# Three feed-forward tiles per down product, and the next block's factors made in steps and kept in HBM

## The chip, the cores and the metric

The kernel runs on one core of a Trainium2 chip. The metric is the device time of one execution in microseconds; the time given for a kernel is the median of its runs.

## The reference

One layer of a hybrid encoder trunk on 2048 tokens of width 1024: three token mixers and their output projection, then a gated feed-forward part with a convolution of width 3 over tokens. The change lies in the feed-forward part alone:

```python
D_MODEL = 1024
SEQ = 2048
D_FF = ((8 * D_MODEL // 3 + 127) // 128) * 128      # 2816, 22 tiles of 128
CONV_W = 3
...
def conv_glu_ffn(h, w_up, conv_w, conv_b, w_down):
    gate, val = jnp.split(h @ w_up, 2, axis=-1)
    t = gate.shape[1]
    gp = jnp.pad(gate, ((0, 0), (CONV_W - 1, 0), (0, 0)))
    conv = conv_b
    for i in range(CONV_W):
        conv = conv + gp[:, i:i + t] * conv_w[i]
    return (jax.nn.silu(conv) * val) @ w_down
...
        x = x + jnp.concatenate([ya, yb, yc], axis=-1) @ w_out[l]
        h = rms_norm(x, ffn_norm_g[l])
        x = x + conv_glu_ffn(h, w_up[l], conv_w[l], conv_b[l], w_down[l])
```

## The kernel before

The first stages (projections, the three mixers, the output projection) fill the first 1780 us or so. They leave x + mixers in HBM as x2D, features by tokens, and the inverse norms of all tokens in the tiles rsb. The feed-forward stage (line 1258 on) follows.

Tokens are worked in three blocks, `BL` (line 58): twice 344, then twice 340 and twice 340 tokens; the two halves of a block are the two halves of a Strassen-like scheme. Each f32 operand is split into a high and a low part (`split`, line 159: a cast on ScalarE to the high part, a subtraction on VectorE, or on another engine if one is named, for the low part), and each product of two operands is three matmuls: high-high, high-low, low-high.

Per block the right factors `Bs` (seven tiles B0 to B6, each of four row sets, high and low) hold sums and differences of the normalised x. `build` (line 1166) makes them: per row set j it scales two x tiles on VectorE (line 1172), takes four sums or differences on GpSimd (lines 1177 to 1180), and splits seven results into the B tiles (line 1182). It is a generator that yields after each split. The B tiles have one buffer each.

The loop (line 1356) runs over 22 tiles of 128 gate and 128 value columns. `up_w` loads a tile's weights into two of three raw buffers and makes four combined ones on GpSimd, a tile ahead. `ffn_up` (line 1289) takes seven products in the order 0, 1, 6, 2, 3, 4, 5, each 12 matmuls into one PSUM bank; before each product its weights are split into a wu tile (four buffers). VectorE combines the products; then come the convolution (lines 1320 and 1322), the silu, the gating (line 1324) and the split of the result into a hid tile.

`ffn_down` (line 1336) multiplies hid tiles by w_down for eight output tiles and two halves, a PSUM bank each, and adds each bank to acc on VectorE (line 1346). It takes G = 2 tiles at a time: after tiles 2, 4, ..., 18 the two earliest ready ones. `down_w` (line 1329) loads w_down rows into a raw buffer and splits them into a wd tile (two buffers), the low part on GpSimd. After the last tile, four are left: two groups of two, and the weights of the second group are loaded after the first group's products.

At the end of a block (lines 1369 to 1387) `build` for the next block runs interleaved with these last two groups, `PACE` = 1 step per output bank. Then acc goes to the output, and the next block loads its acc from x2D. All loads and stores of this stage are issued by SP.

The order of instructions on an engine is not that of the code: a scheduler places an instruction when its operands and buffers are there by its own reckoning, earlier code first. The semaphores follow from that order.

## Time and profile before

| | us |
|---|---|
| median of 3 runs (3209.77 to 3211.91) | 3211.55 |
| the profiled execution: its time | 3213.01 |
| its span | 3211.2 |
| TensorE busy (94%) | 3017.4 |
| VectorE busy (74%) | 2368.5 |
| ScalarE busy (43%) | 1394.9 |
| GpSimd busy (30%) | 950.1 |

The profile is one execution, recorded instruction by instruction. Its engines are PE (TensorE matmuls), PEld (TensorE weight loads, beside PE), DVE (VectorE), ACT (ScalarE), POOL (GpSimd) and SP, which issues most DMAs. A group of instructions is told by its line in the kernel, the engine, the operation, and out<-in by the program's names; "x132" is a count. Behind an arrow stands what ended the idle time before the instruction. The lines 160 and 161 belong to `split`, so there the tile's name tells which split it is. A window gives, for a stretch of the span, its length, the busy time of PE, PEld, DVE, ACT and POOL with their instruction counts, the granted TensorE clock as a share of full speed, the share of time in which the DMA engines were busy, and GB/s. Times are us from the span's start unless marked otherwise.

### The profile page before, as it was taken

What the parts mean: (1) busy time and instruction counts of PE and PEld (TensorE: products, weight loads), DVE (VectorE), ACT (ScalarE), POOL (GpSimd) and SP (SyncE); (2) the same over time, 40 slices, a digit from 0 to 9 for tenths busy, and PEclk for the clock granted to TensorE, in tenths of its full rate; (3) what the DMA queues carried; (4) which work ended last, traced back from release to release, by engine and by line L of the source; (5) the groups of instructions that cost most, each with busy time, mean ns of one, the idle gap of its engine ahead of it and who ended that gap; (6) DMA issues with size and microseconds to landing.
All of it is one profiled execution on the core that took longest, in us unless ns stands there. A gap on an engine that the chain in (4) does not pass through costs nothing.

```text
span 3211.2 us, 49128 instructions
## 1 busy us (share of the span) xinstructions
PE 3017.4 (94%) x17820; PEld 2638.9 (82%) x17820; DVE 2368.5 (74%) x4590; ACT 1394.9 (43%) x2610; POOL 950.1 (30%) x928
## 2 busy tenths in 40 slices
PE   6988989998999979999989999999999998999999
PEld 4766767776767756677789899998899998999998
DVE  6667666756676646777553788889988889988886
ACT  5434444544444335578532343334333334333332
POOL 1010010001001021144242444444444444444443
PEclk8988999999999989999999999999999999999999
DMA  7756755656644576523234322222422222422221
GB/s 223 213 154 179 207 165 150 175 151 177 171 120 125 143 177 152 139 73 86 73 103 151 132 79 80 79 69 77 158 79 80 79 79 81 136 73 79 79 80 68
DMA packets 310818, 392.92 MB, mean 122 GB/s; under 512 B 137144, under 2 KB 228804, under 8 KB 299752
## 3 DMA queue, kind: packets, MB, share of 16 engines
q1 hardware_dynamic: 305936, 378.44, 40.0%
q0 software_dynamic: 2816, 8.39, 0.9%
q10 hardware_dynamic: 1824, 2.95, 0.4%
q8 instruction: 141, 2.31, 0.3%
q14 instruction: 101, 0.83, 0.1%
HBM read 304.65 MB, written 86.36 MB: 122 GB/s over the span
## 4 chain that ended last, share of the span: by engine, by line
PE 67%; DVE 17%; issue 5%; ACT 4%; DMA 4%; POOL 2%; SPq 1%; POOLq 0%; DVEq 0%; ACTq 0%
PE ps L1299 7%; PE ps L1298 7%; PE ps L1297 7%; PE ps L1345 4%; PE ps L1343 4%; PE ps L1344 4%; PE mm L282 2%; PE mm L281 2%; PE mm L283 2%; PE o L1069 2%; DVE tm L533 2%; DVE T L536 2%; PE z L652 2%; PE ps L1205 2%; PE ps L1206 2%
## 5 line engine op out<-in xcount | busy, mean ns | idle before, releaser
L1299 PE MATMUL ps<-B,wu 128*128 128x340 f32 (+1 forms) x1848 | 594.0, 321 | 19.6 <-DVE wu L161 19.4
L1297 PE MATMUL ps<-B,wu 128*128 128x340 f32 (+1 forms) x1848 | 589.7, 319 | 1.9 <-ACT wu L160 1.8
L1298 PE MATMUL ps<-B,wu 128*128 128x340 f32 (+1 forms) x1848 | 590.5, 320 | 0.0
L1299 PEld LDWEIGHTS ps<-B,wu 128*128 128x128 f32 x1848 | 348.7, 189 | 27.9 <-DVE wu L161 27.5
L1343 PE MATMUL ps<-hid,wd 128*128 128x340 f32 (+1 forms) x1056 | 341.9, 324 | 13.4 <-ACT wd L160 10.2
L1297 PEld LDWEIGHTS ps<-B,wu 128*128 128x128 f32 x1848 | 348.7, 189 | 2.6 <-ACT wu L160 2.1
L1298 PEld LDWEIGHTS ps<-B,wu 128*128 128x128 f32 x1848 | 347.8, 188 | 0.1
L1345 PE MATMUL ps<-hid,wd 128*128 128x340 f32 (+1 forms) x1056 | 338.8, 322 | 3.8 <-POOL wd L161 3.7
L1344 PE MATMUL ps<-hid,wd 128*128 128x340 f32 (+1 forms) x1056 | 340.1, 322 | 0.0
L281 PE MATMUL mm<-hT,w 128*128 128x512 f32 x704 | 314.5, 447 | 22.4 <-ACT w L160 16.0
L161 DVE TENSOR_TENSOR wu<-S,wu 128x512 fp32r<-128x512 f32 x264 | 258.0, 984 | 74.3 <-ACT wu L160 74.3
L282 PE MATMUL mm<-hT,w 128*128 128x512 f32 x704 | 291.2, 414 | 7.8 <-DVE hT L161 6.6
L283 PE MATMUL mm<-hT,w 128*128 128x512 f32 x704 | 291.3, 414 | 1.2 <-DVE w L161 1.1
L1346 DVE TENSOR_TENSOR acc<-acc,ps 128x340 f32<-128x340 f32 (+1 forms) x528 | 247.1, 502 | 48.1 <-PE ps L1345 47.8
L161 POOL TENSOR_TENSOR wd<-raw,wd 128x1024 fp32r<-128x1024 f32 x66 | 171.3, 2618 | 269.4 <-ACT wd L160 267.8
L160 ACT CAST wu<-S 128x512 fp32r<-128x512 f32 x264 | 162.9, 618 | 151.2 <-PE ps L1299 140.7
L1343 PEld LDWEIGHTS ps<-hid,wd 128*128 128x128 f32 x1056 | 201.6, 191 | 16.4 <-ACT wd L160 11.1
L1345 PEld LDWEIGHTS ps<-hid,wd 128*128 128x128 f32 x1056 | 201.6, 191 | 6.1 <-POOL wd L161 6.1
L161 DVE TENSOR_TENSOR wu<-raw,wu 128x512 fp32r<-128x512 f32 x198 | 201.1, 1017 | 5.6 <-ACT wu L160 5.6
L1344 PEld LDWEIGHTS ps<-hid,wd 128*128 128x128 f32 x1056 | 201.8, 191 | 0.0
L281 PEld LDWEIGHTS mm<-hT,w 128*128 128x128 f32 x704 | 138.8, 197 | 66.9 <-ACT w L160 17.0
L160 ACT CAST wu<-raw 128x512 fp32r<-128x512 f32 x198 | 120.7, 620 | 162.0 <-PE ps L1299 142.1
(337 smaller groups left out, 6814.2 us busy)
## 6 DMA issues: line engine op xcount, KB each, us to landing
w<-wD SPq DMA_DIRECT2D x72, 1024.0 KB, 6.6
raw<-in_w_up_dram SPq DMA_DIRECT2D x132, 512.0 KB, 3.6
raw<-in_w_down_dram SPq DMA_DIRECT2D x66, 512.0 KB, 3.6
wD<-w SPq DMA_DIRECT2D x24, 1024.0 KB, 5.5
wraw<-in_w_in_dram SPq DMA_DIRECT2D x24, 512.0 KB, 6.3
xt<-in_xT_dram SPq DMA_DIRECT2D x48, 256.0 KB, 4.2
K<-qkD SPq DMA_DIRECT2D x21, 512.0 KB, 8.3
Q<-qkD SPq DMA_DIRECT2D x84, 128.0 KB, 2.9
```

The source lines that it names most:

```text
L160: (hi_eng or nc.scalar).copy(hi, src) if (hi_eng or nc.scalar) is nc.scalar else hi_eng.tensor_copy(out=hi, in_=src)
L161: (lo_eng or nc.vector).tensor_tensor(lo, src, f(hi), op=ALU.subtract)
L281: mm(ps, hi[:, kt, 0:P], hT[kt][:, 0, :], start=(kt == 0), stop=False)
L282: mm(ps, hi[:, kt, 0:P], hT[kt][:, 1, :], start=False, stop=False)
L283: mm(ps, lo[:, kt, 0:P], hT[kt][:, 0, :], start=False, stop=(kt == KT - 1))
L1297: mm(ps, whl[:, 0, kt, :], Bs[p][:, kt, 0, 0:n], start=(kt == 0), stop=False)
L1298: mm(ps, whl[:, 0, kt, :], Bs[p][:, kt, 1, 0:n], start=False, stop=False)
L1299: mm(ps, whl[:, 1, kt, :], Bs[p][:, kt, 0, 0:n], start=False, stop=(kt == 3))
L1343: mm(ps, wd[:, 0, ch], hid[:, 0, cs], start=(u == 0), stop=False)
L1344: mm(ps, wd[:, 0, ch], hid[:, 1, cs], start=False, stop=False)
L1345: mm(ps, wd[:, 1, ch], hid[:, 0, cs], start=False, stop=(u == G - 1))
L1346: nc.vector.tensor_tensor(acc[ct][:, cs], acc[ct][:, cs], ps, op=ALU.add)
```

## The change

`ffn_down` takes three tiles a group: tiles 0 to 2, ..., 15 to 17, then 18 and 19, and 20 and 21. A bank collects nine matmuls instead of six before it is added to acc. A group's down products follow the up products of the next group's first tile, so four tiles of up products come first in a block, then three between two down groups. wd has three buffers. The last pair's w_down is split into four wu tiles (`down_last`) instead of wd tiles.

The next block's factors are no longer built at the block's end into the B tiles. `build_ahead` makes them in small steps within the running block, from its third tile on, up to three steps per tile (before the matmuls of products 1, 2 and 4 of `ffn_up`), 48 steps in all: one step loads x tiles, two scale one each, two do two GpSimd operations each in x and in a tile that shares its buffer with TS, and seven split one result each into a tile st (two buffers) and store it in HBM (`kept`). At the block's end, when each B tile's last product is through, seven DMAs load the factors from HBM, in the order in which the products use them. x4 has two buffers instead of three, TS grows to 688 columns, and the scratch for DMA descriptors shrinks.

```diff
-BUFS = {"fr": 7, "bk": 4, "bp": 2, "fl": 6, "wraw": 2, "w": 3, "xt": 2, "pr": 3, "p2": 6, "vs": 1, "st": 4, "raw": 3, "yh": 5, "xr": 3, "tmp": 5, "wu": 4, "s4": 4, "hid": 4, "x4": 3, "vv": 1}
+BUFS = {"fr": 7, "bk": 4, "bp": 2, "fl": 6, "wraw": 2, "w": 3, "xt": 2, "pr": 3, "p2": 6, "vs": 1, "st": 4, "raw": 3, "yh": 5, "xr": 3, "tmp": 5, "wu": 4, "s4": 4, "hid": 4, "x4": 2, "vv": 1}
...
-    TSR = [(cA0.tile([P, 640], F32, name="TS"), cA0.tile([P, 256], F32, name="TR"))]
+    TSR = [(cA0.tile([P, 2 * HN], F32, name="TS", tag="TS")[:, 0:640], cA0.tile([P, 256], F32, name="TR"))]
...
-    wd4 = p4.enter_context(tc.tile_pool(name="wd4", bufs=2))
+    wd4 = p4.enter_context(tc.tile_pool(name="wd4", bufs=3))
...
-    G = 2
+    st4 = p4.enter_context(tc.tile_pool(name="st4", bufs=2))
+
+    GROUPS = [list(range(g, g + 3)) for g in range(0, NF - 4, 3)] + [[NF - 4, NF - 3], [NF - 2, NF - 1]]
...
+    def build_ahead(b, kept):
+
+        t1, n = BL[b]
+
+        def put(p, j, o):
+            t = st4.tile([P, 2, HN], F32R, name="st")
+            split(t[:, 0, 0:n], t[:, 1, 0:n], o)
+            nc.sync.dma_start(out=kept[p][:, j], in_=f(t[:, :, 0:n]))
+
+        for j in range(4):
+            hs = []
+            for kt in (j, j + 4):
+                h = x4.tile([P, 2 * HN], F32, name="x4")
+                nc.sync.dma_start(out=h[:, 0 : 2 * n], in_=x2D[kt * P : (kt + 1) * P, t1 : t1 + 2 * n])
+                hs.append(h)
+            yield
+            for kt, h in zip((j, j + 4), hs):
+                nc.vector.scalar_tensor_tensor(
+                    h[:, 0 : 2 * n], h[:, 0 : 2 * n], par("ffn_g", kt), rsb[b][:, 0 : 2 * n], op0=ALU.mult, op1=ALU.mult
+                )
+                yield
+            b11, b12, b21, b22 = hs[0][:, 0:n], hs[0][:, n : 2 * n], hs[1][:, 0:n], hs[1][:, n : 2 * n]
+            tt = cA0.tile([P, 2 * HN], F32, name="tt", tag="TS")
+            t2, t3 = tt[:, 0:n], tt[:, HN : HN + n]
+            nc.gpsimd.tensor_tensor(t3, b22, b12, op=ALU.subtract)
+            nc.gpsimd.tensor_tensor(t2, t3, b11, op=ALU.add)
+            yield
+            for p, o in ((0, b11), (1, b21), (2, t2)):
+                put(p, j, o)
+                yield
+            nc.gpsimd.tensor_tensor(b12, b12, b11, op=ALU.subtract)
+            nc.gpsimd.tensor_tensor(b21, t2, b21, op=ALU.subtract)
+            yield
+            for p, o in ((3, t3), (5, b22), (4, b12), (6, b21)):
+                put(p, j, o)
+                yield
 
...
-    def ffn_up(Bs, left, fi, n):
+    def ffn_up(Bs, left, fi, n, work):
...
+            if p in (1, 2, 4):
+                next(work, None)
...
-        return wd
+        return lambda s, ct: wd[:, s, ct * P : (ct + 1) * P]
+
+    def down_last(fis):
+
+        raws = []
+        for fi in fis:
+            raw = raw4([P, DM])
+            nc.sync.dma_start(out=raw, in_=w_down[fi * P : (fi + 1) * P, :])
+            raws.append(raw)
+        whl = [[ws4.tile([P, 2, 4, P], F32R, name="wu") for _ in fis] for h in range(2)]
+        for u, raw in enumerate(raws):
+            for h in range(2):
+                t = whl[h][u]
+                split(t[:, 0], t[:, 1], raw[:, h * 512 : h * 512 + 512].rearrange("p (a c) -> p a c", c=P), None, nc.gpsimd)
+        return [lambda s, ct, u=u: whl[ct // 4][u][:, s, ct % 4, :] for u in range(len(fis))]
 
     def ffn_down(acc, grp, n):
         for ct in range(KT):
-            ch = slice(ct * P, (ct + 1) * P)
             for hf in range(2):
                 cs = slice(hf * n, hf * n + n)
                 ps = bank()[:, 0:n]
                 for u, (hid, wd) in enumerate(grp):
-                    mm(ps, wd[:, 0, ch], hid[:, 0, cs], start=(u == 0), stop=False)
-                    mm(ps, wd[:, 0, ch], hid[:, 1, cs], start=False, stop=False)
-                    mm(ps, wd[:, 1, ch], hid[:, 0, cs], start=False, stop=(u == G - 1))
+                    mm(ps, wd(0, ct), hid[:, 0, cs], start=(u == 0), stop=False)
+                    mm(ps, wd(0, ct), hid[:, 1, cs], start=False, stop=False)
+                    mm(ps, wd(1, ct), hid[:, 0, cs], start=False, stop=(u == len(grp) - 1))
                 nc.vector.tensor_tensor(acc[ct][:, cs], acc[ct][:, cs], ps, op=ALU.add)
-                yield
 
     left_ = None
     for b, (t0, n) in enumerate(BL):
@@ -1352,39 +1405,34 @@
         acc = [a4.tile([P, 2 * HN], F32, name=f"acc{ct}") for ct in range(KT)]
         for ct in range(KT):
             nc.sync.dma_start(out=acc[ct][:, 0 : 2 * n], in_=x2D[ct * P : (ct + 1) * P, ts_])
-        ready, work = [], iter(())
+        work, more = iter(()), b + 1 < len(BL)
+        if more:
+            n1 = BL[b + 1][1]
+            kept = [dram.tile([P, 4, 2, n1], F32, name=f"BD{b}{p}") for p in range(7)]
+            work = build_ahead(b + 1, kept)
+        hids, g = {}, 0
         for fi in range(NF):
             left = left_ if left_ is not None else up_w(fi)
-            ready.append(ffn_up(Bs, left, fi, n))
+            hids[fi] = ffn_up(Bs, left, fi, n, work if fi > 1 else iter(()))
             if todo is not None:
                 todo()
                 todo = None
-            left_ = up_w((fi + 1) % NF) if fi + 1 < NF or b + 1 < len(BL) else None
-            if G < len(ready) and fi < NF - G:
-                for _ in ffn_down(acc, list(zip(ready, wds)), n):
-                    pass
-                ready = ready[G:]
-            if fi % G == 0 and fi < NF - G:
-                wds = [down_w(fi + u) for u in range(G)]
-        if b + 1 < len(BL):
-            t1, n1 = BL[b + 1]
-
-            def load(kt, t1=t1, n1=n1):
-                xt = x4.tile([P, 2 * HN], F32, name="x4")
-                nc.sync.dma_start(out=xt[:, 0 : 2 * n1], in_=x2D[kt * P : (kt + 1) * P, t1 : t1 + 2 * n1])
-                return xt
-
-            Bs = factors()
-            work = build(Bs, b + 1, load, tmp4)
-        while ready:
-            for _ in ffn_down(acc, list(zip(ready, wds)), n):
-                for _ in itertools.islice(work, PACE):
-                    pass
-            ready = ready[G:]
-            if ready:
-                wds = [down_w(NF - G + u) for u in range(G)]
+            left_ = up_w((fi + 1) % NF) if fi + 1 < NF or more else None
+            if fi == 0:
+                wds = [down_w(k) for k in GROUPS[0]]
+            elif g + 2 < len(GROUPS) and fi == GROUPS[g + 1][0]:
+                ffn_down(acc, [(hids.pop(k), w) for k, w in zip(GROUPS[g], wds)], n)
+                g += 1
+                wds = [down_w(k) for k in GROUPS[g]]
         for _ in work:
             pass
+        wdl = down_last(GROUPS[-1])
+        if more:
+            Bs = factors()
+            for p in (0, 1, 6, 2, 3, 4, 5):
+                nc.sync.dma_start(out=f(Bs[p][:, :, :, 0:n1]), in_=kept[p])
+        for ks, ws_ in zip(GROUPS[-2:], (wds, wdl)):
+            ffn_down(acc, [(hids.pop(k), w) for k, w in zip(ks, ws_)], n)
...
-    nc = _bacc.Bacc("TRN2", target_bir_lowering=False, num_devices=1, dynamic_dma_scratch_size=4096)
+    nc = _bacc.Bacc("TRN2", target_bir_lowering=False, num_devices=1, dynamic_dma_scratch_size=1024)
```

## Rows read from the trace of the kernel before

**Rows 1.** the page, part 1: engine, busy us (share), instructions
```profile
PE 3017.4 (94%) x17820; PEld 2638.9 (82%) x17820; DVE 2368.5 (74%) x4590; ACT 1394.9 (43%) x2610; POOL 950.1 (30%) x928
```

**Rows 2.** windows, feed-forward: stretch, its us, busy us per engine, PEclk, DMA
```profile
1850.00:2200.00 350.00, 350.00 (x2222) 350.00 (x2221) 299.14 (x435) 135.93 (x203) 164.59 (x121) 1.00 0.24 79
...
2800.00:3180.00 380.00, 380.00 (x2440) 380.00 (x2440) 326.88 (x482) 148.34 (x223) 168.78 (x126) 1.00 0.22 74
```

**Rows 3.** windows at the ends and starts of the three blocks
```profile
1780.00:1831.60 51.60, 44.42 (x256) 42.12 (x255) 44.25 (x58) 23.58 (x41) 26.83 (x18) 0.93 0.53 184
2179.70:2221.50 41.80, 40.44 (x254) 39.76 (x253) 36.50 (x45) 19.82 (x33) 24.76 (x19) 1.00 0.23 76
2221.50:2264.80 43.30, 36.36 (x193) 33.84 (x191) 40.42 (x65) 16.38 (x31) 21.69 (x20) 0.88 0.45 144
2264.90:2313.80 48.90, 42.21 (x253) 39.34 (x254) 47.76 (x57) 19.63 (x32) 27.19 (x19) 1.00 0.48 153
2657.90:2699.50 41.60, 40.15 (x254) 39.31 (x253) 36.42 (x45) 19.72 (x33) 24.73 (x19) 1.00 0.23 77
2699.50:2742.50 43.00, 35.57 (x194) 33.37 (x193) 40.12 (x65) 16.37 (x31) 22.40 (x20) 0.88 0.41 133
2742.50:2788.50 46.00, 41.32 (x254) 39.20 (x253) 43.59 (x54) 19.63 (x32) 25.04 (x19) 1.00 0.47 150
...
3132.60:3171.90 39.30, 39.30 (x254) 39.30 (x253) 33.02 (x46) 17.66 (x28) 19.90 (x13) 1.00 0.20 68
3171.90:3207.10 35.20, 32.30 (x193) 31.18 (x191) 19.03 (x36) 4.49 (x5) 4.89 (x3) 0.95 0.17 65
```

**Rows 4.** waits of PE from 2221.5 to 2264.8: who, us in total, times, longest
```profile
PE ps L1343 <- ACT wd L160: 4.8, 1, 4.8
```

**Rows 5.** groups on DVE, 2803.5 to 3180: count, busy us, mean ns, idle before
```profile
L1346 DVE TENSOR_TENSOR acc<-acc,ps 128x340 f32<-128x340 f32 x137 | 63.2, 501 | 9.8 <-PE ps L1345 9.8
```

**Rows 6.** timeline of DVE: start us, us, what [idle before]; two follow-on tiles
```profile
2762.62 2.78 DVE L1322 SCALAR_TENSOR_TENSOR cv<-gt,pps,cv 128x680 f32<-128x680 f32 x2
...
2777.89 2.80 DVE L1322 SCALAR_TENSOR_TENSOR cv<-gt,pps,cv 128x680 f32<-128x680 f32 x2 [0.43 <-ACT cv L1320]
```

**Rows 7.** timeline of DVE, last block: a split for the third follow-on tile
```profile
3159.14 0.68 DVE L161 TENSOR_TENSOR wu<-raw,wu 128x512 fp32r<-128x512 f32 x1
```

**Rows 8.** groups on DVE, 2200 to 2300: work on the next factors
```profile
L161 DVE TENSOR_TENSOR B<-u,B 128x340 fp32r<-128x340 f32 x16 | 13.7, 858 | 2.7 <-ACT B L160 2.7
...
L161 DVE TENSOR_TENSOR B<-x,B 128x340 fp32r<-128x340 f32 x12 | 10.5, 885 | 0.0
L1172 DVE SCALAR_TENSOR_TENSOR x<-x,pps,rsb 128x680 f32<-128x680 f32 x8 | 10.4, 1314 | 0.0
```

**Rows 9.** timeline of all engines from 2203.3: a POOL and a DVE row
```profile
2204.17 1.29 POOL L1286 TENSOR_TENSOR S<-raw,S 128x512 f32<-128x512 f32 x1 [1.48 <-DVE wu L161]
...
2204.37 1.64 DVE L161 TENSOR_TENSOR wu<-raw,wu 128x512 fp32r<-128x512 f32 x1
```

**Rows 10.** timeline of SP's DMA issues, block 0
```profile
1803.73 1.38 SPq L1374 DMA_DIRECT2D x<-x2D  x3
```

**Rows 11.** windows with DMA near its most
```profile
1800.00:1805.00 5.00, 5.00 (x32) 4.81 (x31) 4.53 (x10) 2.29 (x4) 0.58 (x1) 1.00 1.01 384
...
2750.00:2760.00 10.00, 10.00 (x67) 10.00 (x66) 8.77 (x13) 3.26 (x5) 6.59 (x5) 1.00 0.91 274
```

**Rows 12.** timeline of all engines, 2275 to 2283: a load and its cast
```profile
2275.55 0.33 SPq L1331 DMA_DIRECT2D raw<-in_w_down_dram  x1
...
2281.78 1.05 ACT L160 CAST wd<-raw 128x1024 fp32r<-128x1024 f32 x1 [3.31 <-DMA raw<-in_w_down_dram]
```

**Rows 13.** waits of SP's DMA queue, 1850 to 3211
```profile
SPq L1279 <- POOL wd L161: 473.5, 57, 15.6
```

**Rows 14.** the list of DMA issues: count, KB each, median us to landing
```profile
raw<-in_w_down_dram SPq DMA_DIRECT2D x66, 512.0 KB, 3.6
...
yD<-yl POOLq DMA_DIRECT2D x16, 256.0 KB, 3.7
```

## Prediction

> **What bounds the kernel now.** I read the page first: TensorE is busy for 94% of the span, VectorE for 74% [rows 1], so the question is where TensorE is not fed. The windows answer it: inside a token block of the feed-forward stage TensorE is busy for every microsecond, and the matmul counts give its pace, 350/2222 = 0.1575 us for 344 columns and 380/2440 = 0.1557 us for 340 [rows 2]. VectorE works 299 and 327 us of those 350 and 380 us (85 to 86%) and nobody waits for it there. The losses lie at the block ends. Three tiles' up products are 252 matmuls (39.7 us in block 0, 39.2 us after), the last four tiles' down products 192 (30.2 and 29.9 us). Against that the stretches of [rows 3] took, in order of time: block 0's first three tiles 51.6, 11.9 over; block 0's last three 41.8, 2.1 over; its last downs 43.3, 13.1 over; block 1's first three 48.9, 9.7 over; block 1's last three 41.6, 2.4 over; its last downs 43.0, 13.1 over; block 2's first three 46.0, 6.8 over; block 2's last three 39.3, 0.1 over; the closing downs 35.2, 5.3 over. Together 64.4 us, of which the two changes of block hold 24.9 and 22.3. Within the downs one wait of 4.8 us is for a cast of w_down [rows 4], which needs a buffer that the group before still reads; after it the granted clock of the stretch is 0.88. The rest is VectorE: busy 40.4 of 43.3 us and 47.8 of 48.9 us [rows 3], because it makes the next block's factors there.
>
> **The change, part by part.** (1) *Groups of three.* PSUM groups fall from 11 x 16 to 8 x 16 a block, so 3 x 48 = 144 additions to acc go, each 63.2/137 = 0.46 us [rows 5]: 66 us of VectorE. All of it lies beside down matmuls, where TensorE is full; credit 0. The price is that three tiles' up products now follow each other without a down between (four at a block's start). When VectorE sets the pace, one tile takes 2777.89 - 2762.62 = 15.27 us [rows 6] against 84 x 0.1557 = 13.08 us of matmuls, so it falls back 2.2 us a tile. What covers this is the lead of up to four split weights (wu has four buffers), 48 x 0.1557 = 7.5 us. How thin it gets, block 2's last three tiles show: the split for the third tile's second product ends at 3159.82 [rows 7], and TensorE, started at 3132.6, wants it at 3132.6 + 15 x 12 x 0.1557 = 3160.6. That run lost only 0.1 us, but its last tile prepares no following one. Block 2's five runs of three: between 0.1 and 2.2 each; I take 0.6, near the row that is most like them: 3 us. Block 0's fourth tile in its opening: between 0 and 2.2, since VectorE already sets the pace there; I take 1.5.
>
> (2) *Factors made in the running block.* Per block 28 splits (13.7 and 10.5 us) and 8 scalings of 1.31 us [rows 8]: 34.7 us of VectorE, besides 28 ScalarE casts and 16 GpSimd operations, twice. The nearest row is a run of three tiles that carried a quarter of it: blocks 0 and 1 already split one set of seven factors, with its four GpSimd operations, into their last three tiles, and these lost 2.1 and 2.4 us where the run without it lost 0.1 [rows 3]. Four sets a block at 2.25 make 9 us, 18 us for two blocks. Below, 0, if it falls into VectorE's free seventh; above, the first rival.
>
> The steps' 28 stores and the 7 loads add SP issues, 0.33 us each for a plain one [rows 12]. SP waits a lot: up to 15.6 us for a raw buffer [rows 13]. A store queued behind such a wait holds one of two st buffers; the third step's cast then waits on ScalarE, and the weight casts behind it, and then TensorE. A wait under the 7.5 us of lead costs nothing, the longest one 8 us. How often it meets a store the trace can't show; I take 0, since the stores are at least a product apart, and leave it in the range.
>
> (3) *The changes of block.* The last three tiles carry no step (48 steps, three a tile from the third, end with tile 17): 1 instead of 2.1 and 2.4, gain 2.5. In the last downs VectorE keeps only 32 additions, and the last pair's weights go to wu buffers, so the 4.8 us wait goes. Late next is the second of its raw loads or the seven factors. The factors are 7 x 1.39 = 9.75 MB, 25.4 us at 384 GB/s, 35.6 us at 274 [rows 11]; the first may start when tile 21's first product is through, 72 matmuls or 11.2 us before the downs, and the last is wanted some 11 us after them. So there are 52 us for 26 to 36. I take 2 us lost each, instead of 13.1: gain 22.2. Bounds 0 and the second rival.
>
> The next block's first tiles start without a backlog on VectorE, but with half the lead, because two of the four wu buffers come free only with the last down, and with four tiles in a row: I take 4 us each for 9.7 and 6.8, gain 8.5; bounds 0 and those rows.
>
> (4) *The end.* Its downs lose 1 instead of 5.3: gain 4.3, bounds 0 and 5.3. TS grown to 688 columns and x4 at two buffers: nothing waits for them. The smaller descriptor scratch can touch only the GpSimd-queue DMAs before this stage, such as the 16 of yD at 3.7 us [rows 14]; each has long before its reader comes; 0, at most one such landing.
>
> **The sum.** Gains 2.5 + 22.2 + 8.5 + 4.3 = 37.5; costs 3 + 1.5 + 18 = 22.5; net 15. The profiled execution took 3213.0 us, 1.5 above the median of 3211.55, so 3198 beside it and **3197** as a median. Its own range, with each taken value moved halfway to its bounds, is 3185 to 3207.
>
> **Rivals.** *A: VectorE is overrun in the runs of three.* Per run it falls back 3 x 2.2 = 6.6 us, and a fifth of 34.7 is 6.9 more. It decides from the point where the sum passes the 7.5 us of lead: 13.5 - 7.5 = 6.0 us in each of ten runs, 60 us instead of 18, the bare runs 0 instead of 3: 3197 + 39 = **3236**, slower. For it: the thin lead [rows 7] and GpSimd's part. A split that met a GpSimd operation took 1.64 us [rows 9], one that met none 0.68 [rows 7]; the change moves 16 such operations a block among the splits. The Trainium skill, SBUF — State Buffer, section Who interferes with whom, states that a VectorE instruction with two SBUF inputs contends with a GpSimd instruction that reads SBUF; by that rule, which the two rows agree with, spreading the steps can't hide them for free. It also covers the case that the change doesn't do what it says: instructions are not issued in the code's order (block 1's first x loads, due at its block's end, went out at 1803.73 [rows 10], over 400 us early), so the steps may bunch in the first seven tiles. Then VectorE has 7 x 15.27 + 16 x 0.46 + 34.7 = 149 us of work there, TensorE 7 x 13.08 + 22.4 = 114; less 7.5 of lead that is 27.5 a block instead of 9, again 3234. Against it: the runs with a quarter of the steps lost 2.1 and 2.4, not 6.
>
> *B: the last weight load queues behind the factors.* The second raw of the last pair can load only when the first is split, about the end of tile 21; by then most factor loads are out. If it lands after them, that is 25.4 to 35.6 us after a start 11.2 us before the downs, plus about 4 us for its own load, cast and first split: 18 to 28 us into the downs, wanted at 14.9. A stall of 3 to 13, 8 on the mean, and some 3 more at the lower clock as in [rows 3], 11 instead of 2, twice: 3197 + 18 = **3215**. For it: a w_down load issued among others at 2275.55 was cast at 2281.78 [rows 12], 6.2 us, where 3.6 is the median [rows 14]. The Trainium skill, DMA: Bandwidth & Descriptors, section Queues, rings and completion order, says that on each engine descriptors are consumed in ring order; by that rule, which those rows agree with, a load issued after the factors can't pass them. Against it: SP may issue it after four of the seven.
>
> *C: everything is covered.* The steps and bare runs cost 0 (21 us less) and the starts 2 instead of 4: **3172**.
>
> **How the numbers follow.** Chances: forecast 0.40, A 0.28, B 0.17, C 0.15. A measurement of this kernel tells 0.2%, 6.4 us, from no change, so faster means below 3205.1 and slower above 3218. Faster: 0.34 of the forecast, all of C, 0.04 of B: 0.53. Same: 0.05, 0.03 of A, 0.08 of B: 0.16. Slower: 0.01, 0.25 of A, 0.05 of B: 0.31. The range reaches from C to A, 3172 to 3238.
>
> **What would show it.** Windows of the changes of block: final downs near 32 us and first tiles losing some 4 us would show step 3 right; a TensorE wait for a wd or wu cast in the second half of the downs, with the factor loads still running, is B. Inside blocks 0 and 1 TensorE should lose 2 to 3 us per run to VectorE's splits; 6 in each, or long losses in the first seven tiles alone, is A. Block 2 without steps separates the price of the runs from that of the steps. The forecast is wrong if ScalarE waits for stores, or if TensorE waits for a factor's load at a block's start.

## Result and profile after

The changed kernel takes 3245.4 us (median of 4 runs, 3239.6 to 3247.8), the kernel before on the same chip 3211.7; the ratio is 1.0098, 95% interval 1.0078 to 1.0117. That is 1.0% slower, clear of the noise, and outside the forecast's range, on the side of rival A. The profiled run took 3239.6 us with a span of 3237.8, 26.6 us above before's.

The page's first part of after; it answers [rows 1]:

```profile
PE 3027.8 (94%) x17820; PEld 2638.8 (81%) x17820; DVE 2344.8 (72%) x4446; ACT 1385.7 (43%) x2616; POOL 975.6 (30%) x934
```

VectorE has the 144 instructions fewer (4590 - 4446) that the groups of three promised, 66 us by [rows 5], but its busy time fell by 23.7 only.

Windows of after, columns as in [rows 2] (stretch, its us, busy us of PE, PEld, DVE, ACT, POOL with counts, granted clock, DMA share, GB/s). The first two answer [rows 2], the others [rows 3]:

```profile
1850.00:2200.00 350.00, 328.12 (x2023) 319.48 (x2022) 297.16 (x404) 133.50 (x217) 170.12 (x127) 1.00 0.35 112
2800.00:3180.00 380.00, 374.03 (x2377) 370.11 (x2377) 312.26 (x423) 141.21 (x217) 173.20 (x126) 1.00 0.23 75
...
1783.80:1851.00 67.20, 58.47 (x338) 56.28 (x339) 62.02 (x84) 34.21 (x59) 43.51 (x29) 0.95 0.59 197
1873.60:1931.60 58.00, 44.84 (x255) 40.99 (x254) 53.49 (x66) 25.37 (x46) 37.60 (x27) 0.97 0.52 158
1954.30:2004.10 49.80, 42.77 (x254) 39.60 (x253) 44.12 (x54) 21.97 (x39) 33.65 (x23) 1.00 0.45 148
2026.70:2067.50 40.80, 40.26 (x255) 39.80 (x253) 37.34 (x43) 19.80 (x32) 28.47 (x19) 1.00 0.27 91
2258.50:2289.00 30.50, 30.50 (x194) 30.50 (x193) 20.89 (x40) 4.97 (x8) 5.77 (x6) 1.00 0.95 325
2289.00:2354.60 65.60, 56.22 (x338) 53.47 (x337) 57.17 (x63) 27.55 (x45) 35.48 (x25) 0.97 0.41 141
2731.60:2761.40 29.80, 29.80 (x193) 29.80 (x193) 20.43 (x40) 4.94 (x8) 5.72 (x6) 1.00 0.98 330
2761.40:2827.20 65.80, 58.77 (x338) 55.86 (x337) 56.94 (x63) 27.55 (x45) 35.06 (x25) 0.92 0.41 142
3203.90:3234.00 30.10, 30.10 (x193) 29.83 (x192) 19.40 (x36) 3.04 (x4) 2.20 (x3) 1.00 0.19 76
```

Read from below: the three last downs take 30.5, 29.8 and 30.1 us with TensorE full, where [rows 3] had 43.3, 43.0 and 35.2. This part did better than forecast: the factor loads, and the stores and loads of acc behind them, move 325 and 330 GB/s beside the downs, and TensorE waits for none of them. But TensorE is no longer full inside the blocks. The first three stretches of ups of block 0 (tiles 0 to 3, 4 to 6, 7 to 9) take 67.2, 58.0 and 49.8 us for 52.9, 39.7 and 39.7 us of matmuls, and the fourth is nearly clean, 40.8. The four-tile openings of blocks 1 and 2 take 65.6 and 65.8 us for 52.3.

What TensorE waits for in the whole stage is nearly one thing, VectorE's splits of the up weights (waits of PE, 1780 to 3238: who, us in total, times, longest):

```profile
PE ps L1340 <- DVE wu L161: 51.7, 66, 3.6
PE ps L1338 <- ACT wu L160: 3.9, 3, 2.1
PE ps L1338 <- ACT st L160: 2.0, 1, 2.0
```

The waits make 57.6 of the 88 us that the ledger below counts. The rest lies in matmuls that took longer than the pace of [rows 2]: TensorE is busy for 1394.3 us in the stage for 1362 us of matmuls at that pace. Some of this falls into stretches with a lower granted clock, as the openings above (0.92 to 0.97).

The store line of the steps (engine, operation, count: ns min/median/max, first and last start in us) says when the steps ran:

```profile
L1283 SPq DMA_DIRECT2D BD<-st x56: 359/365/676, 1735.1 to 1989.0; - x56
```

All 56 stores, those for block 2 too, were out by 1989.0, within block 0's first ten tiles; the first went out in the stage before. Block 1 carried no step at all. In that earlier stage TensorE is busy for 2.9 us less between 1720 and 1760 (row of after, then of before):

```profile
1720.00:1760.00 40.00, 37.15 (x225) 36.08 (x224) 17.89 (x29) 12.95 (x30) 15.05 (x15) 0.96 0.80 253
1720.00:1760.00 40.00, 40.00 (x254) 39.34 (x253) 11.84 (x20) 10.66 (x23) 11.02 (x12) 1.00 0.55 172
```

There it waits 2.9 us for GpSimd's additions in the tile rsb. Whether a step delayed them, no run shows.

**The ledger.** For each stretch of ups or downs, its length less its matmuls at the pace of [rows 2]. The stage is 1362 us of matmuls plus these sums. "Runs" are all other ups and downs (the downs among them 0.7 below the pace in both kernels).

```
us over the matmuls    opening   openings   runs   last    sum   median   ratio to before
                       block 0   1 and 2           downs                  (95% interval)
before                   11.9       16.4      5.2   31.7    65.2   3211.7
after                    14.3       26.8     46.8    0.4    88.3   3245.4   1.0098 (1.0078-1.0117)
e1 no steps              11.0       27.5     21.2    0.4    60.1   3207.8   0.9991 (0.9977-1.0006)
e2 steps in place        15.3       28.9     71.7    0.3   116.2   3262.7   1.0156 (1.0132-1.0180)
e3 groups alone          11.6       29.8     28.6   24.3    94.3   3242.7   1.0095 (1.0070-1.0120)
e4 ahead alone           12.9       19.5     57.8    0.3    90.5   3238.5   1.0073 (1.0048-1.0097)
e5 steps in downs        11.0       25.9     25.8    0.4    63.0   3212.1   1.0005 (0.9985-1.0025)
e6 e5, late w_down       10.2       25.7     25.6    0.4    61.8   3208.3   0.9982 (0.9965-0.9999)
e7 e5, late acc          11.2       18.2     25.7    0.4    55.5   3202.0   0.9967 (0.9948-0.9987)
e8 e5, both               9.5       18.1     24.5    0.4    52.4   3203.4   0.9971 (0.9951-0.9990)
e9 e7 in twos            10.0       12.2      6.9    0.4    29.4   3179.5   0.9895 (0.9873-0.9917)
e10 e9, six wu            3.5        2.6     22.1    0.2    28.4   3178.8   0.9892 (0.9869-0.9915)
e11 twos, in place       10.4       11.8     32.4    0.3    54.9   3198.5   0.9956 (0.9942-0.9970)
e12 e2, three st         13.2       27.6     72.2    0.0   113.0   3265.6   1.0167 (1.0143-1.0190)
e13 e11, four st         10.0       12.0     31.6    0.3    53.9   3200.9   0.9957 (0.9942-0.9972)
e14 e2, three u          14.0       28.7     70.3    0.2   113.2   3262.6   1.0161 (1.0133-1.0189)
e15 e11, no stores       11.6       12.3     14.5    0.1    38.4   3185.3   0.9912 (0.9883-0.9941)
e16 e11, no GpSimd       10.8       12.0     19.9    0.4    43.0   3189.5   0.9925 (0.9897-0.9954)
e17 e2, no stores        14.5       30.9     69.4    0.4   115.2   3256.0   1.0132 (1.0091-1.0173)
e18 e2, no GpSimd        12.3       28.0     61.5    0.3   102.1   3246.9   1.0104 (1.0066-1.0142)
```

From before to after: last downs -31.4, openings 1 and 2 +10.4, block 0's opening +2.4 and its next two runs +28.4, the other runs of three 19.2 where before had 5.9. That is +23.1; with the 3.8 us by which the stage began later, and 0.3 less at its end, it is the difference of the spans. The sums are better than the medians for comparing: the kernels begin this stage between 1772 and 1788 us, even those that are the same up to there.

### The profile page after: what moved, and what is told of

The parts are those of the page before. It is cut to its first block, busy times and chain, and to the rows that moved or that the text cites. A ratio compares the mean times of both kernels' runs of the same rounds, so it can differ in the third digit from the quotient of the medians.

```text
span 3237.8 us, 49195 instructions
## 1 busy us (share of the span) xinstructions
PE 3027.8 (94%) x17820; PEld 2638.8 (81%) x17820; DVE 2344.8 (72%) x4446; ACT 1385.7 (43%) x2616; POOL 975.6 (30%) x934
## 4 chain that ended last, share of the span: by engine, by line
PE 50%; DVE 27%; issue 8%; ACT 6%; DMA 6%; POOL 2%; SPq 0%; DVEq 0%; ACTq 0%; POOLq 0%
DVE wu L161 7%; PE ps L1399 5%; PE ps L1397 5%; PE ps L1398 5%; PE mm L281 3%; PE mm L283 3%; PE mm L282 3%; PE o L1069 2%; PE ps L1340 2%; DVE tm L533 2%; DVE cv L1365 2%; PE z L652 2%; DVE T L536 2%; PE ps L1339 2%; PE ps L1338 2%
## 5 line engine op out<-in xcount | busy, mean ns | idle before, releaser
L161 DVE TENSOR_TENSOR wu<-S,wu 128x512 fp32r<-128x512 f32 x264 | 296.7, 1129 | 50.1 <-ACT wu L160 49.4
L1399 PE MATMUL ps<-hid,wd 128*128 128x340 f32 (+1 forms) x960 | 306.1, 319 | 0.0
L1397 PE MATMUL ps<-hid,wd 128*128 128x340 f32 (+1 forms) x960 | 305.7, 318 | 0.0
L1398 PE MATMUL ps<-hid,wd 128*128 128x340 f32 (+1 forms) x960 | 305.5, 318 | 0.0
L1400 DVE TENSOR_TENSOR acc<-acc,ps 128x340 f32<-128x340 f32 (+1 forms) x384 | 188.4, 505 | 139.4 <-PE ps L1399 139.4
L161 POOL TENSOR_TENSOR wd<-raw,wd 128x1024 fp32r<-128x1024 f32 x60 | 153.5, 2586 | 261.5 <-ACT wd L160 261.4
L1397 PEld LDWEIGHTS ps<-hid,wd 128*128 128x128 f32 x960 | 180.6, 188 | 0.0
L1398 PEld LDWEIGHTS ps<-hid,wd 128*128 128x128 f32 x960 | 180.5, 188 | 0.0
L1399 PEld LDWEIGHTS ps<-hid,wd 128*128 128x128 f32 x960 | 180.3, 188 | 0.0
```

The costliest lines, as they stand in the source:

```text
L161: (lo_eng or nc.vector).tensor_tensor(lo, src, f(hi), op=ALU.subtract)
L1397: mm(ps, wd(0, ct), hid[:, 0, cs], start=(u == 0), stop=False)
L1398: mm(ps, wd(0, ct), hid[:, 1, cs], start=False, stop=False)
L1399: mm(ps, wd(1, ct), hid[:, 0, cs], start=False, stop=(u == len(grp) - 1))
L1400: nc.vector.tensor_tensor(acc[ct][:, cs], acc[ct][:, cs], ps, op=ALU.add)
```

## Experiments: which part costs what

**Theory and rivals.** After the result the theory was: the steps are issued when their inputs are ready and not where the code asks, so they bunch, and VectorE is overrun (rival A). Rivals: the steps are dear wherever they lie; or the groups of three are the loss.

**e1.** The steps and the factor loads are left out; blocks 1 and 2 then use block 0's factors.

```diff
-            work = build_ahead(b + 1, kept)
+            work = iter(())
 ...
-            Bs = factors()
-            for p in (0, 1, 6, 2, 3, 4, 5):
-                nc.sync.dma_start(out=f(Bs[p][:, :, :, 0:n1]), in_=kept[p])
+            pass
```

> Leaves out the steps that make the factors of blocks 1 and 2, and the factor loads; both blocks use block 0's factors again. If the early bunched steps are what costs, block 0's first ten tiles lose about 14 us over their matmuls instead of 43, the stage starts 4 us earlier, and the time is about 3245 - 31 - 4 = 3210 us; the starts of blocks 1 and 2 should still lose some 13 us each if late weights cause that, and about 5 if the factor loads do. If the runs of three are themselves the cost, the time stays above 3230.

3207.8 us, ratio 0.9991: the change without its steps is as fast as before, no faster. The steps cost 28.2 us of the ledger. The openings of blocks 1 and 2 lose 27.5 us without any step or factor load, and the runs of three 0.7 to 1.6 each, the very last 0.1.

**e2.** Each step is held, in issue order, behind the split where the code calls it.

```diff
-            split(whl[:, 0], whl[:, 1], left[p])
+            last = split(whl[:, 0], whl[:, 1], left[p])
             if p in (1, 2, 4):
-                next(work, None)
+                with tc.issue_after(last.ins), tc.issue_after(here[0].ins):
+                    next(work, None)
```

> Every step is held, in issue order only, behind the weight split at which the code asks for it, and its loads behind the current tile's weight load. Steps spread over tiles 2 to 17 of their own block: if the price of the forecast holds (a quarter of a block's steps costs a run of three 2.25 us), the two blocks pay 18 us instead of 35: about 3228 us. If VectorE is overrun in the runs of three (6 us per run with steps), 3245 - 35 + 60 = 3270. If VectorE has the room in between the runs, steps cost nothing more: 3210.

Slower still, 3262.7. Spread as the diff meant them, the steps make the ten runs that hold them lose 4.9 to 8.2 us each, 6.3 on the mean, against 1.0 to 1.5 for the bare runs beside them: rival A's 6.0, not the forecast's 2.25. The openings of blocks 0 and 1, which hold six steps each, lose 15.3 and 16.3 us, that of block 2, which holds none, 12.6. So bunching was not what made the steps dear: bunched they cost the runs 25.6 us against e1, spread 50.5. Where VectorE's 56 splits of the steps start tells the two apart. Bunched, 14 start in the stage before, 13 beside downs and 29 beside ups; spread, 10 beside downs and 46 beside ups.

**e3 and e4** split the change: e3 is the kernel before with groups of three (three w_down buffers, the small scratch, x4 at two), e4 the changed kernel with groups of two (and two w_down buffers).

```diff
     G = 2
+    GROUPS = [list(range(g, g + 3)) for g in range(0, NF - 4, 3)] + [[NF - 4, NF - 3], [NF - 2, NF - 1]]
```

> The kernel before with groups of three alone (three wd buffers, two x4 buffers, the small descriptor scratch); the next factors are made at the block's end as before. The runs of three of the changed kernel lost 1.1 to 1.5 us each without any step in them; 14 such runs, and four tiles in a row at three starts at 2 us each, give 3211.5 + 18 + 6 = 3236 us less nothing. If the 13 us at the starts belong to four tiles in a row, 3250. If groups of three cost nothing, 3212.

```diff
-    GROUPS = [list(range(g, g + 3)) for g in range(0, NF - 4, 3)] + [[NF - 4, NF - 3], [NF - 2, NF - 1]]
+    GROUPS = [[g, g + 1] for g in range(0, NF, 2)]
```

> The changed kernel with groups of two (two wd buffers): the factors made ahead and the last pair's weights in wu buffers stay. If bunched steps cost 35 us and the starts 13 each for late weights, it loses what the changed kernel does less the runs of three (about 15 us): 3230 us. If groups of three are the main cost, it falls under 3200, since the 31 us gained in the last downs stay.

Each part alone is slower, by 1.0 and 0.7%. The groups of three alone take 7.4 us off the last downs and add 23.4 to the runs and 13.4 to the later openings. Factors made ahead save 31.4 us in the last downs, but with groups of two the steps bunch as well (stores 1837.1 to 2097.2) and runs of two that lost 0.06 us or less lose 6.9 to 9.8 each, and the downs between them 9 us in all.

**e5.** The steps move from the up products to the down products, eight to a group, each behind an addition to acc.

```diff
-            if p in (1, 2, 4):
-                next(work, None)
 ...
-                nc.vector.tensor_tensor(acc[ct][:, cs], acc[ct][:, cs], ps, op=ALU.add)
+                add = nc.vector.tensor_tensor(acc[ct][:, cs], acc[ct][:, cs], ps, op=ALU.add)
+                if hf:
+                    with tc.issue_after(add.ins), tc.issue_after(here[0].ins):
+                        next(work, None)
```

> The changed kernel with the 48 steps of a block moved out of the up products into the down products of the six full groups, eight to a group, each held behind one addition to acc. Theory 1 (a step costs time only where VectorE is already the pace-setter, that is in the runs of up products; beside downs it is free): a group has 144 matmuls, 22.4 us, in which VectorE makes 16 additions, 7.4 us, and would add 34.7/6 = 5.8 us of steps; so the runs of three stay at 40.3 to 41.2 us, the block openings lose 13 to 14 us as they do without steps, and the median is that of the kernel without steps plus the nothing that they cost: 3205 to 3212. Theory 2 (the steps cost what VectorE spends on them, wherever they lie, because its time over a whole block is what is short: 45.8 + 7.4 + 5.8 = 59.0 of 61.6 us per group, and GpSimd beside it): 2 to 5 us per group, twelve groups, 3235 to 3260.

The same 48 steps a block now cost 4.6 us of the ledger's runs in all where in place they cost 50.5; 52 of the 56 splits start beside downs. Windows over block 0's third run of three in e1 (with the downs behind it), the same run in e2, and in e5 with the downs behind it:

```profile
1985.40:2026.20 40.80, 40.26 (x253) 39.70 (x253) 37.43 (x43) 19.72 (x32) 28.25 (x19) 1.00 0.28 91
2026.20:2048.90 22.70, 22.70 (x146) 22.70 (x145) 14.82 (x28) 3.83 (x5) 0.77 (x2) 1.00 0.16 47
```
```profile
2004.80:2052.40 47.60, 42.96 (x254) 41.23 (x253) 43.19 (x48) 21.19 (x37) 33.41 (x23) 0.96 0.32 107
```
```profile
1987.70:2028.80 41.10, 40.30 (x254) 39.72 (x253) 39.86 (x44) 19.77 (x32) 29.04 (x19) 1.00 0.37 118
2028.80:2051.60 22.80, 22.80 (x147) 22.80 (x146) 17.90 (x33) 5.84 (x9) 4.42 (x6) 1.00 0.26 90
```

In the bare run VectorE is busy for 37.4 of 40.8 us, and for 14.8 of the 22.7 us of downs behind it. In e2 it does 43.2 us of work in a run that has 39.7 us of matmuls, and TensorE waits. Beside the downs it is busy for 17.9 of 22.8 us with the steps, and TensorE is full.

## Experiments: the openings

The opening of block 2 in after, SP's issues, then ScalarE, GpSimd and VectorE (start us, us, engine, line, what, idle before and its releaser):

```profile
2762.52 4.00 SPq L1407 DMA_DIRECT2D acc<-x2D  x5
2766.62 1.08 SPq L1318 DMA_DIRECT2D raw<-in_w_up_dram  x2
```
```profile
2773.46 1.89 ACT L160 CAST wu<-raw 128x512 fp32r<-128x512 f32 x3 [5.63 <-DMA raw<-in_w_up_dram]
```
```profile
2781.90 2.86 POOL L161 TENSOR_TENSOR wd<-raw,wd 128x1024 fp32r<-128x1024 f32 x1
...
2786.05 5.63 POOL L161 TENSOR_TENSOR wd<-raw,wd 128x1024 fp32r<-128x1024 f32 x2 [0.23 <-ACT wd L160]
```
```profile
2782.43 3.05 DVE L1363 SCALAR_TENSOR_TENSOR cv<-gt,pps,cv 128x680 f32<-128x680 f32 x1
...
2789.39 2.85 DVE L161 TENSOR_TENSOR wu<-S,wu 128x512 fp32r<-128x512 f32 x1
```

Three suspects: the second tile's weights, issued behind the acc loads; GpSimd's burst of w_down splits, beside which a VectorE split takes 2.85 us (0.68 alone, [rows 7]); VectorE's own pace. The Trainium skill, SBUF — State Buffer, section Who interferes with whom, says that a VectorE instruction with two SBUF inputs contends with a GpSimd one that reads SBUF, and these rows agree; whether that sets the end is another question. e6 takes the burst away (first w_down tiles behind the third tile's preparation), e7 the late weights, e8 both:

```diff
-            if fi == 0:
+            if fi == 2:
                 wds = [down_w(k) for k in GROUPS[0]]
```

> As the kernel with the steps in the downs, and the first group's three w_down tiles of each block loaded, cast and split after the third tile's preparation and no longer after the first's. Theory P (the openings lose their 13.5 us because GpSimd splits three w_down tiles in one burst beside VectorE's splits and stretches them from some 2 to 3 us): the openings lose about 5 us each, 16 to 25 us less in all than with the steps in the downs alone. Theory L (they lose it because the second tile's raw weights are loaded behind the acc loads and arrive late): unchanged within 5 us. Theory V (VectorE's own pace at an opening, 4 tiles at 15.3 us against 13.1, sets it): unchanged, 4 x 2.2 = 9 us remain whatever is moved.

```diff
-        for ct in range(KT):
-            nc.sync.dma_start(out=acc[ct][:, 0 : 2 * n], in_=x2D[ct * P : (ct + 1) * P, ts_])
 ...
+            if fi == 0:
+                with tc.issue_after(here[0].ins):
+                    for ct in range(KT):
+                        nc.sync.dma_start(out=acc[ct][:, 0 : 2 * n], in_=x2D[ct * P : (ct + 1) * P, ts_])
```

> As the kernel with the steps in the downs, and the eight loads of acc of a block issued behind the second tile's weight loads and no longer ahead of them. Theory L: the 5.6 us for which a cast of w_up waits on its load at an opening goes, 5 us for each of blocks 1 and 2, 10 us less in all than with the steps in the downs alone. Theories P and V: unchanged within 4 us, since the lead returns nothing while GpSimd's burst or VectorE's pace comes after it.

> Both of these: acc loads behind the second tile's weights, and the first group's w_down tiles behind the third tile's. If late weights and GpSimd's burst each take a part of the 13.5 us, the openings of blocks 1 and 2 lose 3 to 5 us and block 0's less too: 20 to 28 us below the kernel with the steps in the downs, near 3185. If VectorE's pace sets it, the openings lose 9 us or more, and the time is within 8 us of that kernel.

The burst is innocent at blocks 1 and 2: e6's openings lose 25.7 us for 25.9. The acc loads cost 7.7 us (25.9 to 18.2), and with both moved 18.1 stay, 8.9 and 9.2. Theory V's number is left: 4 tiles at 15.27 us [rows 6] are 61.1, and e7's and e8's openings take 61.1 to 61.8. Block 2's in e8:

```profile
2719.40:2780.90 61.50, 55.20 (x339) 53.75 (x338) 56.02 (x63) 27.88 (x45) 34.81 (x25) 0.97 0.44 146
```

By this sum an opening costs 2.2 us for each tile that it has ahead of its first down, and the groups of three made it four tiles. The pace itself no experiment changes, so this part is argued. VectorE is not full here either (56.0 of 61.5 us): TensorE waits 6.3 us for its splits, and the other 3 us lie in slower matmuls, at a granted clock of 0.97. And e10 below shows that more lead, with the same work for VectorE, takes most of the loss out of openings of three tiles (12.2 to 2.6 us for blocks 1 and 2).

## Experiments: groups of two, and what a step costs among ups

**e9** keeps what e4, e5 and e7 showed: factors ahead, groups of two, steps in the downs (six to a group), acc loads late (the diff is against e7). **e10** gives the third w_down buffer's place to two more wu buffers.

```diff
-    wd4 = p4.enter_context(tc.tile_pool(name="wd4", bufs=3))
+    wd4 = p4.enter_context(tc.tile_pool(name="wd4", bufs=2))
 ...
-    GROUPS = [list(range(g, g + 3)) for g in range(0, NF - 4, 3)] + [[NF - 4, NF - 3], [NF - 2, NF - 1]]
+    GROUPS = [[g, g + 1] for g in range(0, NF, 2)]
 ...
-                if hf:
+                if (2 * ct + hf) % 8 in (1, 4, 6):
```

> The next block's factors made within the running block, but with the groups of two of the kernel before (two w_down buffers), the steps beside the down products, six to a group, and the acc loads behind the second tile's weights. Theory 'a run loses where VectorE has no down to catch up in': runs of two lose nothing (2 x 2.2 = 4.4 us against 7.5 us of lead), where runs of three lose 1.1 to 1.5 each, 17 us in all, and the openings are three tiles long and not four, 2.2 us less each; so 17 + 6 us below the kernel with groups of three, its steps in the downs and its acc loads late: near 3178. Rival 'the 66 us of additions that groups of three save are needed to hold the steps': a group of two takes 26.2 + 15 = 41.2 us of TensorE and 2 x 15.3 + 7.4 + 4.3 = 42.2 us of VectorE, 1.0 us too much, 16 groups with steps, 16 us more: near 3195, and the runs of two of blocks 0 and 1 lose 1 us or more each where those of block 2 lose none.

> As the kernel with groups of two and the steps in the downs, and the place of the third w_down buffer given to two more buffers of split up weights, six and not four. If lead is what an opening lacks, two more products of lead at each block's start, 2 x 12 x 0.1557 = 3.7 us, are saved at the two changes of block and a part of it at the stage's start: 4 to 10 us less than with four. If the openings hang on when the weights arrive, or on GpSimd, and not on lead, no difference beyond 3 us.

e9 takes 3179.5 us, 1.05% below before and 2.0% below the change; it beats both. A run of two with the downs behind it, and block 1's opening:

```profile
2354.90:2381.20 26.30, 26.30 (x171) 26.30 (x170) 24.14 (x32) 13.26 (x22) 19.73 (x12) 1.00 0.41 138
2381.20:2396.10 14.90, 14.90 (x98) 14.90 (x98) 14.89 (x28) 4.34 (x7) 3.59 (x6) 1.00 0.22 71
2251.50:2296.80 45.30, 40.83 (x253) 39.12 (x253) 40.19 (x45) 20.02 (x33) 23.16 (x18) 1.00 0.53 181
```

VectorE is busy for 14.89 of the 14.90 us of downs and TensorE loses nothing. Of the runs of two only the first of block 1 loses time, 2.1 us. The rival's "1.0 us too much per group" didn't show: VectorE is busy for 24.1 + 14.9 = 39.0 of the 41.2 us here, so a tile in a run of two needs less of it than the 15.27 us that an opening takes. e10 is the same time, with its losses elsewhere: its openings lose 6.1 us in all for e9's 22.2, but the downs inside its blocks lose 20.6. There TensorE waits for the additions (PE, 2295 to 2700: who, us in total, times, longest):

```profile
PE ps L1398 <- DVE acc L1401: 3.6, 8, 0.7
PE ps L1398 <- ACT hid L160: 0.6, 1, 0.6
PE ps L1399 <- DVE hid L161: 0.5, 1, 0.5
```

These waits are 4.7 of the 9.2 us that block 1's downs lose. I read it so, and no run tests it: with more free buffers the splits run further ahead in VectorE's queue, and the additions that free PSUM come later. More than the 4 to 10 us expected was gained at the openings (16.1) and given back there.

**e11** puts the steps back among the ups, in groups of two (e9 with e2's edit), to ask what a step costs there.

> The kernel with groups of two and the acc loads late, but with its steps among the up products, three to a tile, each held behind the split where the code asks for it, and not beside the downs. Theory 'lead': a run of two falls back 2 x 2.2 = 4.4 us and its six steps take 6 x 34.7/48 = 4.3 us of VectorE, 8.7 us against 7.5 us of lead, so each of the 16 runs with steps loses about 1.2 us, more by what GpSimd's operations stretch them, 1.2 to 2.5: 19 to 40 us above the same kernel with the steps in the downs, 3199 to 3220, where runs of three with steps in place lost 5 to 8 each. Rival 'a step among up products costs its whole VectorE time whatever the length of the run': 4.3 us in each of 16 runs, 69 us more, 3248. Rival 'only the length of the run matters': no loss, 3180.

19 us above e9, just under the low edge of "lead's" band, and not as it said: every second run loses 2.7 to 4.5 us and the others nothing. Two runs that follow each other in block 1:

```profile
2411.50:2441.20 29.70, 27.26 (x170) 26.13 (x169) 25.71 (x30) 12.58 (x22) 19.46 (x13) 1.00 0.34 107
2456.10:2482.30 26.20, 26.20 (x169) 26.20 (x169) 23.23 (x29) 13.31 (x22) 20.33 (x13) 1.00 0.34 121
```

In the trace the losing run holds three of the steps' splits and one of their GpSimd operations, the clean one a split, two scalings and two GpSimd operations; the rest falls into the downs (the expectations below counted by the code's order, and were off in that). ScalarE's waits (1846 to 2690) offered a cause that the prediction had named and set to 0, a step's cast behind a store, the weight casts queued behind it:

```profile
ACT st L160 <- DMA BD<-st: 101.9, 36, 5.4
```

**e12, e13, e14** give the steps more st buffers: three in e2's kernel (with u at three for room; e14 is the control for that), four in e11's.

```diff
-    u4 = p4.enter_context(tc.tile_pool(name="u4", bufs=4))
+    u4 = p4.enter_context(tc.tile_pool(name="u4", bufs=3))
 ...
-    st4 = p4.enter_context(tc.tile_pool(name="st4", bufs=2))
+    st4 = p4.enter_context(tc.tile_pool(name="st4", bufs=3))
```

> The changed kernel with its steps held in place among the up products of runs of three, and three st buffers where it has two (room made by three buffers for u and not four). Theory S (ScalarE's cast of a step waits up to 5 us for the store that holds the st buffer, and the casts of the up weights are queued behind it): that wait nearly goes, and with it half or more of the 5 to 8 us that each run with steps loses: 1 to 4 us each are left, 3262 less 30 to 50, near 3222. Theory V (the steps cost VectorE's and GpSimd's own time in runs where VectorE sets the pace): the waits on stores go, the runs still lose 5 to 7 each, 3255 to 3265.

> Groups of two, acc loads late, steps held in place among the up products, and four st buffers for two. In the kernel with two st buffers every second run loses 3 to 4 us, always the one that holds four splits with their stores and four GpSimd operations, none the one that holds three splits and two scalings, although the latter is more VectorE work. Theory S: the loss goes altogether, 27 us in the trace, down to the time of the kernel with the steps in the downs, 3180. Theory V or GpSimd's four operations: at least 2 of the 3 to 4 us stay, 3192 to 3200.

> The same with two st buffers: the control for the u buffer that was given up. Within 3 us of the kernel with the steps held in place, 3262.

Nothing moved: 3265.6 beside 3262.6, and 3200.9 for e11's 3198.5. Theory S, that a buffer more frees the casts, falls. Of e11's wait three quarters stay in e13:

```profile
ACT st L160 <- DMA BD<-st: 78.1, 23, 5.3
```

**e15 to e18** leave work out of the steps: the stores and the factor loads (e17 in e2's kernel, e15 in e11's), or the GpSimd operations (e18, e16).

```diff
-            nc.sync.dma_start(out=kept[p][:, j], in_=f(t[:, :, 0:n]))
```

```diff
-            nc.gpsimd.tensor_tensor(t3, b22, b12, op=ALU.subtract)
-            nc.gpsimd.tensor_tensor(t2, t3, b11, op=ALU.add)
+            t2, t3 = b11, b22
 ...
-            nc.gpsimd.tensor_tensor(b12, b12, b11, op=ALU.subtract)
-            nc.gpsimd.tensor_tensor(b21, t2, b21, op=ALU.subtract)
```

> Steps held in place among the up products of runs of three, but their 28 stores a block and the 7 factor loads are left out (blocks 1 and 2 then use block 0's factors, so what they compute is not the reference's); scalings, GpSimd operations, casts and splits of the steps stay. Theory Q (casts of the up weights stand behind a step's cast that waits for a store's landing on ScalarE): the runs with steps lose 1 to 3 us and not 5 to 8, 40 us less, near 3220. Theory W (the steps' own work on VectorE and GpSimd): the runs still lose 4 us or more each, 3245 to 3262.

> Steps held in place among the up products of runs of three, their stores kept, but the 16 GpSimd operations a block left out (the factors t2, t3 and the two differences are wrong, so what blocks 1 and 2 compute is not the reference's). Theory G (GpSimd's operations stretch VectorE's splits and delay the sums of the up weights): the runs that held them lose 2 to 3 us less, some 25 us less in all, near 3237. Theory Q or VectorE's own time: within 10 us of 3262.

> Groups of two, steps in place, stores and factor loads of the next blocks left out (wrong factors in blocks 1 and 2). Theory Q: the 3 to 4 us that every second run loses go, 3178 to 3183. Theory W: 2 us or more of each stay, 3192 to 3200.

> Groups of two, steps in place, stores kept, the 16 GpSimd operations a block left out (wrong factors in blocks 1 and 2). Theory G: the losing runs, which are those that hold the GpSimd operations, lose 1 us or nothing, 3178 to 3187. Theory Q: they lose 3 us as before, 3195 to 3200.

In runs of three the stores are worth 0.3 us of the 6.3 (e17: 6.0), GpSimd's operations 1.0 (e18: 5.3). Of the 5.1 us over a bare run's 1.2 that leaves 3.8 to the scalings, casts and splits themselves, if the two shares add up, which no run tests. And with no store left, ScalarE's casts do not wait less, the wait is now put down to VectorE (same window: e2, then e17, its kernel without stores):

```profile
ACT st L160 <- DMA BD<-st: 75.7, 35, 4.8
ACT st L160 <- DVE st L161: 102.0, 26, 5.1
```

So in runs of three that wait came from where the cast stood in the queue, not from a store that held it up. In runs of two it is otherwise: a losing run loses 3.4 on the mean, without stores 1.2 (e15), without GpSimd's operations 1.9 (e16). The two removals take off 2.2 and 1.5, together more than there was; the shares are not additive there, and how the stores act on a run of two stays open.

## Why the prediction was wrong

**Where the miss lies.** The sum gave 3198 beside the profiled execution, and it took 3239.6, 41.6 us more. By the ledger the runs lost 41.6 us more than before where the sum had 18.5 (3 + 18 - 2.5): 23.1 of the miss. The openings of blocks 1 and 2 lost 10.4 us more where it had a gain of 8.5: 18.9 of it. Block 0's opening is 0.9 and what lies outside the stage 3.5; the last downs did 4.9 better. Without any step (e1) the runs already lose 16.0 us more than before, so of the 23.1 us the bare runs are 15.5 and the steps 7.6.

**The step that failed is the row from which parts 1 and 2 priced a run of ups.** Part 2 took what "the runs with a quarter of the steps lost" [rows 3], 2.1 and 2.4 us, as a price per quarter and multiplied by four. But that run holds no quarter. Block 0's last three tiles in before hold three of the seven splits, the first at 2216.7, 4.8 us before their end, and one of the four GpSimd operations; the others start in the downs behind. And in e4, e9 and e11 the same last run, behind runs of two and with no step in it, loses 1.8 to 2.2 us. The three splits in before, then e9's last run of block 0:

```profile
L161 DVE TENSOR_TENSOR B<-x,B 128x340 fp32r<-128x340 f32 x3 | 3.1, 1063 | 0.0
```
```profile
2179.40:2221.00 41.60, 40.46 (x253) 39.67 (x253) 35.91 (x45) 18.72 (x30) 25.20 (x19) 1.00 0.45 152
```

So 2.1 and 2.4 was nearly all the price of the run itself and not of steps in it. Part 1 took such a run at 0.6, and the 18 us for the factors rested on no row. (Behind runs of three the same last run loses 3.9 and 4.6, in e3.) Measured with the steps where the diff puts them, the ten runs lose 63.3 us, 5.1 each above a bare run (e2). Rival A's sum, 13.5 us behind less 7.5 of lead, gave 6.0 per run, and 6.3 was measured, but that is partly luck: the same sum gives a bare run 0 and an opening of four tiles 1.3, and they lose 1.2 and, with acc late, 9. The same misread row was also the argument against A.

VectorE's free seventh [rows 2], the lower bound of part 2, is an average over ups and downs, and it tells little. Before's runs of two and their downs, in block 2:

```profile
2803.40:2829.60 26.20, 26.20 (x169) 26.20 (x169) 21.50 (x26) 12.60 (x20) 17.82 (x12) 1.00 0.24 81
2829.60:2844.50 14.90, 14.90 (x98) 14.90 (x97) 13.92 (x27) 3.36 (x5) 0.77 (x2) 1.00 0.23 72
```

There the free time lies in the ups (21.5 of 26.2 us busy) and hardly in the downs (13.9 of 14.9). With groups of three it is the other way round: 37.4 of 40.8 and 14.8 of 22.7 in e1. What decided in the runs is where the steps stand: with 46 of the 56 splits beside ups they cost 50.5 us (e2), with 4 of them there 4.6 (e5).

**That the steps would lie where the code calls them** was wrong as well; A's last sentences had it, from [rows 10]. But bunching made them cheaper, not dearer. A's 27.5 us for each block would be 55 for two; between 1783.8 and 2026.7 both blocks' steps together cost 28.4 us in two runs and 2.4 in the opening, and the runs behind them are bare. VectorE is busy for 211.0 of those 242.9 us.

**Runs of three** (0.6 us taken, bound 2.2): 0.7 to 1.6 each with no step beside them (e1). After's bare runs lose 19.2 us in all, where part 1 had 3 for block 2 and counted the rest with the steps. The row it rested on, 0.1 for the last run of before, was the exception: after's own last run loses 0.1 too. That it has no next tile to prepare is not the whole reason, since e3's last run has none either and loses 1.4.

**The openings** (4 us each taken, bounds 0 and 9.7): 13.3 and 13.5, outside the bounds. Two mistakes: the bounds came from openings of three tiles though the text said four, which is 2.2 us more by the pace of [rows 6]; and the acc loads ahead of the second tile's weights, which cost 3.3 and 4.4 (e7), were not among the things late next.

**The last downs and the end** (1 to 2 us left, gains 22.2 and 4.3): 0.4 left in all, gain 31.4. The larger gain could not pay for the rest. Rival B did not come: the last load of w_down went out behind three of the seven factor loads, and its cast began 4.2 us later.

```profile
2260.80 0.33 SPq L1382 DMA_DIRECT2D raw<-in_w_down_dram  x1
```
```profile
2265.03 1.14 ACT L160 CAST wu<-raw 128x512 fp32r<-128x512 f32 x2 [1.31 <-DMA raw<-in_w_down_dram]
```

What a load issued behind all seven would have met, no run tests. **Groups of three** (credit 0 for 66 us of additions) was right in sign: they save work where TensorE had cover, and e9, which takes them back, is 22.5 us below e7.

**SP, ScalarE and the stores** (0 taken): within 0.4 us of a run of three (e12, e17), though the trace's waits spoke for more. For runs of two the stores, with the factor loads, are worth 16.5 us of the ledger (e11 to e15), and how is open.

**The sum's own range**, 3185 to 3207, does not follow from its rule: with each taken value moved halfway to its bounds, all the same way, it is about 3179 to 3238.

## What to carry to other kernels

A free share of an engine is worth nothing until it is known in which stretch it lies: read the windows of ups and downs apart, and put added work where no other engine waits for what stands behind it in the queue. Fewer, longer groups save additions but lengthen the stretches in which the slower engine must live on its lead; when the saved work was covered anyway, that is a loss (29 us of the ledger in e3). Work whose inputs are ready early goes out early unless it is pinned, and pinning helps only where the place is a good one (e5 against e2). Before a row is used as a price, count in the trace what it holds: a run that was taken to hold seven splits held three.

## What was not expected of the hardware

Factor loads of 1.39 MB each, with acc's stores and loads behind them, moved 325 to 330 GB/s beside full matmuls, DMA share 0.95 to 0.98, and TensorE lost 0.2 us at most. A two-input VectorE operation of 680 columns took 3.05 us beside GpSimd's w_down split, one of 512 columns 2.85 us instead of 0.68, and still the openings of blocks 1 and 2 got no shorter when that split was taken out of the way (e6). And a wait of 75.7 us in total that the trace puts down to stores (e2) did not go when there were no stores (e17): 102.0 us, under another name. A releaser named in a profile is a place to test, not a finding.
